# An event loop sets the order of all engines in a two-level matrix product with attention; eight of sixteen steps with seven products in place of seven

## The chip, the cores and the metric

The kernel runs on one core of a Trainium2 chip. The core has a matrix engine (TensorE, PE in the profile, with its weight loads as PEld), a vector engine (VectorE, DVE), a scalar engine (ScalarE, ACT), GpSimd (POOL) and a queue engine (SyncE, SP) that here only issues DMAs. Each engine takes its own instructions in the order of the program, and semaphores make one wait for another. The metric is the time of one execution on the device in microseconds, as a median of several runs.

## The reference

The input is one sequence of 256 tokens with 4096 channels in float32. With the depth of this case only the attention layer runs, and then the final norm:

```python
def attn_branch(xn, w_in, w_out):
    proj = xn @ w_in                       # 256 x 4096 by 4096 x 16384
    q, k, v, g = jnp.split(proj, 4, axis=-1)
    o = stick_breaking_attention(to_heads(q), to_heads(k), to_heads(v))   # 32 heads of 128
    ...
    return (o * jax.nn.silu(g)) @ w_out    # 256 x 4096 by 4096 x 4096

def reference(...):
    h = x
    h = h + attn_branch(rms_norm(h, norm_attn), w_in_attn, w_out_attn)
    return rms_norm(h, final_norm)
```

In the attention every key before a token gets a share of what the keys nearer to the token have left: `sigmoid(z)` times the product of `1 - sigmoid(z)` over the keys between. The reference computes it in log space with a running sum over the keys. Nearly all arithmetic is in the two products with `w_in` and `w_out`, 336 MB of float32 weights that are each used once.

## The kernel before

**Precision.** TensorE works on a float32 format of less precision (F32R in the code). Every operand is therefore split into a high part (a cast on ScalarE, L174) and a low part (the operand less its high part, a subtraction on VectorE, `minus`, L101 and L102), and `mm3` (L402 to L408) makes three matmuls of each product: high by high, high by low, low by high. In this document a *product* is these three matmuls on a block of 128 tokens by 128 channels with 128 channels by 512 columns of weights.

**Units and steps.** A *unit* is a pair of column blocks of 512 each. Units 0 to 15 belong to `w_in`; unit u holds the columns of q and k of two heads in one block and those of the gate and v in the other. Units 16 to 20 belong to `w_out`. A unit runs over the 4096 input channels in 16 *steps* of 256. The weights of a step, four pieces of 128 x 512, lie together in a buffer called `raw` (3 buffers, `RAW_BUFS`), which four DMAs on SP's queue fill (`load`, L147 to L155).

**Seven or eight products.** With two halves of the tokens, two halves of the channels of a step and two column blocks a step is a 2 x 2 by 2 x 2 matrix product of blocks: eight block products, or seven with sums of blocks ahead (Winograd's form of Strassen's scheme). Three kinds of units:

- plain (0, 1 and 16): eight products in every step, four accumulators in PSUM;
- mixed (2 to 15, 17 and 18): seven accumulators that are combined at the unit's end. The steps in `SEVEN` (L41) take seven products, the others eight, which go to four of the seven accumulators (`SEVEN_PARTS` and `EIGHT_PARTS`, L57 to L66);
- single (19 and 20): one column block, four products a step.

Weights come to TensorE in *parts*. A step of eight has two parts of two pieces (1024 columns in the profile's shapes). A step of seven has three such parts and one of one piece (512 columns); ahead of its third part VectorE makes the sums of weights in place, one of 1024 columns at L165 and two of 512 at L168 and L169. `split` (L157 to L177) makes a part's high and low half. There are 5 places for the parts of two (`PAIRS`) and one for those of one piece (`SINGLES`). The token blocks, with their own sums, are built once for `w_in` (`build_xn`, during unit 1) and once for `w_out` (`build_heads`, during unit 16) and stay in SBUF.

**Around the products.** In unit 0 the kernel also reads x for the norm's factor (`x_stats`, L306). Combining the accumulators of a mixed unit takes three copies on ScalarE and seven additions on VectorE (`combine_early` and `combine_late`, L340 to L355); a bank has to be combined before the next unit's first product may write it. While unit u + 1 runs, the two heads of unit u go through their attention: the gate's SiLU (`gate`, L372), transposes (`heads_T`, L390), scores and log-sigmoids (`scores`, L413; four ScalarE operations in a chain at L422 to L425), the running sum as a matmul with a triangle (`weights_of`, L435; two ScalarE operations in a chain at L444 and L445) and the weighted sum of v (`heads_out`, L456). The outputs of the heads go to DRAM (`heads_parts`, L471), as the blocks of unit 16 and after are read from there again. One PSUM bank (`att`) is left for all of this. In units 17 to 20 the finished blocks of the output get the residual and the gain (`evac_out`, L529), and at the end `finish` (L547) scales and stores them.

**What sets the order.** The loop at L671 goes through the parts. Ahead of a part's products it emits the splits of as many later parts as there are places for; behind the last part of a step it runs what a table `todo` holds for this unit and step. The table is written out by hand (L578 to L648): so `heads_T` for head 0 stands at step 2 of the next unit, `scores` at 3, `weights_of` at 5, `heads_out` at 6, `combine_early` at 14 and `combine_late` at 15. The tile framework's scheduler takes the instructions from there and may still move one ahead of another on the same engine.

Of the kernel before, what the change touches and what calls it, by code (L numbers as in the profile page):

```python
# [18 lines left out]
P = 128  # L19
# [21 lines left out]
SEVEN = (2, 4, 6, 8, 10, 12, 13)  # L41
# [3 lines left out]
SINGLES = 1  # L45
# [27 lines left out]

@with_exitstack
def kernel(
# [10 lines left out]
    nc = tc.nc  # L86
# [12 lines left out]
    nc.scalar.preload_act_table_set("natural_log_exp_and_others")  # L99
# [38 lines left out]
    ends, starts = {}, {}  # L138
    for n, p in enumerate(parts):
        for k, (b, *_) in enumerate(p["prods"]):  # L140
            starts.setdefault((p["u"], b), (n, k))
            ends[p["u"], b] = (n, k)


    raw, wh, wl = {}, {}, {}

    def load(q):  # L147
        if q >= len(quads):
            return
        raw[q] = wp.tile([P, 2 * KT, W], F32, tag="raw", name=f"raw{q}", bufs=RAW_BUFS)  # L150
        for k, (w, blocks, s) in enumerate(quads[q]):
            for chunks in ([slice(0, 1), slice(1, 2)] if q == 0 else [slice(0, 2)]):
                to = slice(KT * k + chunks.start, KT * k + chunks.stop)
                for i, c in enumerate(blocks):
                    nc.sync.dma_start(raw[q][:, to, i * CW : (i + 1) * CW], w[c, s][:, chunks, :])  # L155

    def split(n):  # L157
        p = parts[n]
        q = p["quad"]
        if p["i"] == 0 and (n == 0 or parts[n - 1]["quad"] != q):  # L160
            load(q + RAW_BUFS - 1)
        r = raw[q]
        if p["seven"] and p["i"] == 2:

            nc.vector.tensor_tensor(  # L165
                out=r[:, 0:3:2, :], in0=r[:, 0:4:3, :], in1=r[:, 2:3, :].broadcast_to([P, 2, W]), op=ALU.add
            )
            nc.vector.tensor_tensor(out=r[:, 3, :], in0=r[:, 0, :], in1=r[:, 3, :], op=ALU.add)  # L168
            nc.vector.tensor_tensor(out=r[:, 1, :], in0=r[:, 3, :], in1=r[:, 1, :], op=ALU.add)  # L169
        place, size = p["place"], p["size"]  # L170
        tag, bufs = ("w", PAIRS) if size == KT else ("s", SINGLES)
        wh[n] = wp.tile([P, size, W], F32R, tag=tag + "h", name=f"wh{n}", bufs=bufs)
        wl[n] = wp.tile([P, size, W], F32R, tag=tag + "l", name=f"wl{n}", bufs=bufs)
        for c in ([slice(k, k + 1) for k in range(KT)] if n == 0 else [slice(0, size)]):  # L174
            f = r[:, place, :][:, c, :]
            nc.scalar.copy(wh[n][:, c, :], f)  # L176
            minus(wl[n][:, c, :], f, wh[n][:, c, :])  # L177
# [7 lines left out]
    def load_x(i):  # L185
        if i >= NS:
            return
        xs[i] = ap.tile([P, KT, S], F32, tag=("one", "two", "vh", "vl")[i % 4], name=f"xs{i}")
        if i:
            nc.sync.dma_start(xs[i], xT[i])  # L190
            return
        for k in range(KT):
            nc.scalar.dma_start(xs[i][:, k, :], xT[i][:, k, :])
            if k == 0:
                nc.scalar.dma_start(gcol, gain_in)

# [6 lines left out]
    def split_x(i):  # L203

        if i >= NS:
            return
        h, l = new_forms(i, PLAIN_FORMS, "s")
        for c in range(KT):
            g = gcol[:, i * KT + c : i * KT + c + 1]
            hc = h[:, 2 * c : 2 * c + 2, :].rearrange("p a b -> p (a b)")  # L210
            lc = l[:, 2 * c : 2 * c + 2, :].rearrange("p a b -> p (a b)")
            if i == 0:
                nc.vector.tensor_scalar(out=hc, in0=xs[i][:, c, :], scalar1=g, scalar2=None, op0=ALU.mult)  # L213
            else:
                nc.scalar.activation(hc, xs[i][:, c, :], AF.Copy, scale=g)
            nc.vector.scalar_tensor_tensor(  # L216
                out=lc, in0=xs[i][:, c, :], scalar=g, in1=hc.bitcast(F32), op0=ALU.mult, op1=ALU.subtract
            )
        del xs[i]

    def build(i, y, seven, what):

        names = SEVEN_FORMS if i in seven else EIGHT_FORMS
        h, l = new_forms(i, names, what)
        tt = nc.vector.tensor_tensor

        def both(to, f):
            nc.scalar.copy(h[:, to, :], f)
            minus(l[:, to, :], f, h[:, to, :])

        if names is EIGHT_FORMS:
            both(slice(0, 4), y)
            y4 = y.rearrange("p (a b) c -> p a b c", a=KT)
            tt(out=y4[:, :, 0, :], in0=y4[:, :, 0, :], in1=y4[:, :, 1, :], op=ALU.subtract)
            both(slice(4, 6), y4[:, :, 0, :])
            return
        both(slice(0, 1), y[:, 0:1, :])
        both(slice(1, 3), y[:, 2:4, :])
        tt(out=y[:, 3, :], in0=y[:, 1, :], in1=y[:, 3, :], op=ALU.subtract)
        tt(out=y[:, 1, :], in0=y[:, 0, :], in1=y[:, 1, :], op=ALU.subtract)  # L240
        tt(out=y[:, 0, :], in0=y[:, 3, :], in1=y[:, 0, :], op=ALU.subtract)
        tt(out=y[:, 2, :], in0=y[:, 2, :], in1=y[:, 0, :], op=ALU.add)
        both(slice(3, 7), y)
# [3 lines left out]
    def load_xn(i):  # L247
        if i < NS:
            ys[i] = wp.tile([P, 4, P], F32, tag="gh", name=f"xn{i}", bufs=3)
            nc.gpsimd.dma_start(ys[i].rearrange("p a b -> p (a b)"), xT[i].rearrange("p a b -> p (a b)"))  # L250

    def build_xn(i):
        y = ys.pop(i)
        for c in range(KT):
            yc = y[:, 2 * c : 2 * c + 2, :]
            nc.vector.scalar_tensor_tensor(
                out=yc, in0=yc, scalar=gcol[:, i * KT + c : i * KT + c + 1], in1=rs["rows"],
                op0=ALU.mult, op1=ALU.mult,
            )
        build(i, y, SEVEN, "n")  # L260

    load_x(0)
    load(0)
    load_x(1)
    load(1)
    load_x(2)


    idle = ap.tile([P, W], BF16, tag="qkh", name="idle")
# [6 lines left out]
    make_identity(nc, ident)  # L276
# [14 lines left out]
    nc.vector.tensor_copy(neg_tri, tri_f)  # L291
# [14 lines left out]
    def x_stats(i):  # L306
        t, q = divmod(i, NQ)
        w = D // NQ
        xr = wp.tile([P, w], F32, tag="gh", name=f"xr{i}", bufs=3)
        nc.sync.dma_start(xr, x[t * P : (t + 1) * P, q * w : (q + 1) * w])  # L310
        junk = ap.tile([P, w], F32, tag="qkl", name=f"junk{i}")
        nc.scalar.activation(junk, xr, AF.Square, accum_out=ssq_x[:, t, q : q + 1])

    def x_factor():
        tot = cp.tile([P, NT], F32, name="ssq_xt")
        nc.vector.reduce_sum(tot, ssq_x, axis=AX.X)
        nc.vector.tensor_scalar(out=tot, in0=tot, scalar1=1.0 / D, scalar2=EPS, op0=ALU.mult, op1=ALU.add)
        r = cp.tile([P, NT], F32, name="rin_r")
        nc.scalar.activation(r, tot, AF.Ln)
        nc.scalar.activation(r, r, AF.Exp, scale=-0.5)  # L320
        rs["v"] = cp.tile([P, NT], F32, name="rin_v")
        for t in range(NT):
            c = slice(t, t + 1)
            e = newton(r[:, c], tot[:, c], f"rin{t}")
            nc.vector.tensor_tensor(out=rs["v"][:, c], in0=r[:, c], in1=e, op=ALU.mult)
    def x_rows():

        wide = ap.tile([P, NT, P], F32, tag="qkh", name="wide")
        for t in range(NT):
            nc.vector.tensor_scalar(  # L330
                out=wide[:, t, :], in0=ident, scalar1=0.0, scalar2=rs["v"][:, t : t + 1], op0=ALU.mult, op1=ALU.add
            )
        turned = att.tile([P, NT, P], F32, tag="att", name="turned")
        for t in range(NT):
            nc.tensor.transpose(turned[:, t, :], wide[:, t, :], ident)
        rs["rows"] = ap.tile([P, NT, P], F32, tag="al", name="rows", bufs=2)
        nc.scalar.copy(rs["rows"], turned)


    def combine_early(bank, one, two):  # L340

        tt = nc.vector.tensor_tensor
        nc.scalar.copy(two[:, 0, :], bank[1])
        nc.scalar.copy(one[:, 0, :], bank[1])
        tt(out=two[:, 0, :], in0=bank[6], in1=two[:, 0, :], op=ALU.add)
        tt(out=two[:, 1, :], in0=bank[7], in1=two[:, 0, :], op=ALU.add)
        nc.scalar.copy(one[:, 1, :], two[:, 1, :])

    def combine_late(bank, one, two):
        tt = nc.vector.tensor_tensor  # L350
        for t, b in enumerate((2, 4)):
            tt(out=one[:, t, :], in0=bank[b], in1=one[:, t, :], op=ALU.add)  # L352
        for t in (1, 0):
            tt(out=two[:, t, :], in0=bank[5], in1=two[:, t, :], op=ALU.subtract)
        tt(out=two[:, 0, :], in0=bank[3], in1=two[:, 0, :], op=ALU.add)  # L355
# [4 lines left out]
    def new_heads(u):  # L360

        st["qk", u] = ap.tile([P, NT, W], F32, tag="one", name=f"qk_sb{u}")
# [369 lines left out]
```

## Time and profile before

| what | before |
|---|---|
| time, median of 3 runs | 1788.64 us (1787.94 to 1792.77) |
| the profiled execution's own time | 1787.47 us |
| its span, first to last instruction | 1785.8 us |
| mean granted clock of TensorE | 0.996 |
| instructions | 23623 |
| moved by DMA | 388.81 MB |

The span is a little shorter than the time of the same execution, since the time also holds what lies around the first and the last instruction. Times in the rows are microseconds, or ns where a row says "mean ns"; L102 is line 102 of the kernel; `wl<-raw,wh` names what an instruction writes and reads, with buffer numbers left out. `wh` and `wl` are the high and low parts of weights; `sh`, `nh`, `oh`, `ph` and `rh` with their low parts are the token blocks of units 0 and 1, of the mixed units of `w_in`, of unit 16, of the units after it and of the last steps.

### The profile page before, as it was taken

The numbers are of one execution on the slowest core, as the hardware profiler recorded it, in microseconds if no ns is written. First come the engines' busy times: TensorE is split into PE (matmuls) and PEld (weight loads), VectorE is DVE, ScalarE is ACT, GpSimd is POOL, SyncE is SP. The second block draws the span as 40 slices with busy tenths as digits, with TensorE's granted clock in tenths as the row PEclk, the third lists the DMA queues.
The fourth block names the chain that finished last, engine by engine and source line by source line (L and its number), as shares of the span: only waits on it lengthen the run. The fifth ranks groups of instructions, "written<-read, shape, count | busy, mean of one in ns | idle before, by whom it ended". The sixth has DMA issues, their size and how long they took to land.

```text
span 1785.8 us, 23623 instructions
## 1 busy us (share of the span) xinstructions
PE 1765.1 (99%) x8059; PEld 1456.9 (82%) x8059; DVE 1539.7 (86%) x1885; ACT 1122.8 (63%) x1533; POOL 68.5 (4%) x135
## 2 busy tenths in 40 slices
PE   9999999999999999999999999999999999999997
PEld 7887888888888888888888888888888878888886
DVE  6678999989898989899999999989989888999863
ACT  6665666666666666666666666666666666665543
POOL 0001000000000000000000000000002201000000
PEclk9999999999999999999999999999999999999998
DMA  9966666566666666666666666757578978778874
GB/s 314 339 196 217 197 187 212 183 212 186 209 195 200 205 198 205 198 207 196 210 194 212 193 209 189 221 174 229 170 223 266 308 231 248 228 225 264 258 239 157
DMA packets 373993, 388.81 MB, mean 218 GB/s; under 512 B 23856, under 2 KB 351792, under 8 KB 373872
## 3 DMA queue, kind: packets, MB, share of 16 engines
q1 hardware_dynamic: 357296, 352.15, 62.7%
q0 software_dynamic: 14992, 32.78, 5.8%
q10 hardware_dynamic: 1584, 2.38, 0.4%
q8 instruction: 63, 1.03, 0.2%
q14 instruction: 58, 0.48, 0.1%
HBM read 370.43 MB, written 16.78 MB: 217 GB/s over the span
## 4 chain that ended last, share of the span: by engine, by line
PE 81%; issue 7%; DVE 4%; DMA 4%; ACT 3%; SPq 1%; POOL 0%; ACTq 0%; POOLq 0%; DVEq 0%
PE acc L406 26%; PE acc L407 26%; PE acc L408 25%; DVE wl L102 2%; ACT wh L176 2%; DMA xr<-in_x_dram 1%; DMA raw<-in_w_in_dram 1%; SPq L155 1%; PE tr L395 1%; DMA raw<-in_w_out_dram 1%; DMA xn<-in_xT_dram 0%; DVE raw L165 0%; DMA xres<-in_x_dram 0%; PE o L407 0%; PE o L408 0%
## 5 line engine op out<-in xcount | busy, mean ns | idle before, releaser
L102 DVE TENSOR_TENSOR wl<-raw,wh 128x1024 fp32r<-128x1024 f32 (+1 forms) x865 | 973.9, 1150 | 190.1 <-ACT wh L176 182.8
L176 ACT CAST wh<-raw 128x1024 fp32r<-128x1024 f32 (+1 forms) x865 | 833.5, 992 | 440.1 <-DVE raw L165 127.5
L406 PE MATMUL acc<-wh,nh 128*128 128x512 f32 x1694 | 669.0, 395 | 0.9 <-DVE qk_sb L352 0.6
L407 PE MATMUL acc<-wl,nh 128*128 128x512 f32 x1694 | 660.5, 390 | 0.0
L408 PE MATMUL acc<-wh,nl 128*128 128x512 f32 x1694 | 660.3, 390 | 0.0
L408 PEld LDWEIGHTS acc<-wh,nl 128*128 128x128 f32 x1694 | 318.0, 188 | 67.4
L407 PEld LDWEIGHTS acc<-wl,nh 128*128 128x128 f32 x1694 | 318.6, 188 | 63.7 <-DVE wl L102 2.8
L406 PEld LDWEIGHTS acc<-wh,nh 128*128 128x128 f32 x1694 | 318.1, 188 | 63.8 <-ACT wh L176 1.0
L165 DVE TENSOR_TENSOR raw<-raw 128x1024 f32<-128x1024 f32 x112 | 136.4, 1218 | 0.1
L407 PE MATMUL acc<-wl,ph 128*128 128x512 f32 x314 | 122.5, 390 | 0.4 <-DVE wl L102 0.2
L408 PE MATMUL acc<-wh,pl 128*128 128x512 f32 x314 | 122.2, 389 | 0.0
L406 PE MATMUL acc<-wh,ph 128*128 128x512 f32 x314 | 122.2, 389 | 0.0
L406 PE MATMUL acc<-wh,sh 128*128 128x512 f32 x256 | 100.3, 392 | 0.6 <-DVE sh L213 0.6
L408 PE MATMUL acc<-wh,sl 128*128 128x512 f32 x256 | 99.7, 390 | 0.6 <-DVE sl L216 0.6
L407 PE MATMUL acc<-wl,sh 128*128 128x512 f32 x256 | 99.9, 390 | 0.3 <-DVE wl L102 0.3
L168 DVE TENSOR_TENSOR raw<-raw 128x512 f32<-128x512 f32 x112 | 77.2, 689 | 2.7
L169 DVE TENSOR_TENSOR raw<-raw 128x512 f32<-128x512 f32 x112 | 76.9, 687 | 1.8
L407 PEld LDWEIGHTS acc<-wl,ph 128*128 128x128 f32 x314 | 58.9, 188 | 13.7 <-DVE wl L102 1.7
L406 PEld LDWEIGHTS acc<-wh,ph 128*128 128x128 f32 x314 | 58.9, 188 | 12.4
L408 PEld LDWEIGHTS acc<-wh,pl 128*128 128x128 f32 x314 | 58.9, 188 | 12.1
L406 PEld LDWEIGHTS acc<-wh,sh 128*128 128x128 f32 x256 | 48.1, 188 | 11.0 <-issue 1.4
L408 PEld LDWEIGHTS acc<-wh,sl 128*128 128x128 f32 x256 | 48.0, 188 | 11.1 <-DVE sl L216 1.1
(158 smaller groups left out, 1436.0 us busy)
## 6 DMA issues: line engine op xcount, KB each, us to landing
raw<-in_w_in_dram SPq DMA_DIRECT2D x1020, 256.0 KB, 4.5
raw<-in_w_out_dram SPq DMA_DIRECT2D x256, 256.0 KB, 4.4
xr<-in_x_dram SPq DMA_DIRECT2D x16, 256.0 KB, 4.8
xn<-in_xT_dram POOLq DMA_DIRECT2D x16, 256.0 KB, 3.9
spill_f<-gated POOLq DMA_DIRECT2D x16, 256.0 KB, 3.8
spill_h<-oh POOLq DMA_DIRECT2D x16, 256.0 KB, 3.2
spill_l<-ol POOLq DMA_DIRECT2D x16, 256.0 KB, 2.5
oh<-spill_h POOLq DMA_DIRECT2D x16, 256.0 KB, 4.9
```

The costliest lines, as they stand in the source:

```text
L102: nc.vector.tensor_tensor(out=out_, in0=full, in1=part.bitcast(F32), op=ALU.subtract)
L155: nc.sync.dma_start(raw[q][:, to, i * CW : (i + 1) * CW], w[c, s][:, chunks, :])
L165: nc.vector.tensor_tensor(out=r[:, 0:3:2, :], in0=r[:, 0:4:3, :], in1=r[:, 2:3, :].broadcast_to([P, 2, W]), op=ALU.add)
L168: nc.vector.tensor_tensor(out=r[:, 3, :], in0=r[:, 0, :], in1=r[:, 3, :], op=ALU.add)
L169: nc.vector.tensor_tensor(out=r[:, 1, :], in0=r[:, 3, :], in1=r[:, 1, :], op=ALU.add)
L176: nc.scalar.copy(wh[n][:, c, :], f)
L395: nc.tensor.transpose(tr[:, k, t * P : (t + 1) * P], st["qk", u][:, t, c : c + P], ident)
L406: nc.tensor.matmul(out_, ah, bh, start=start, stop=False, **kw)
L407: nc.tensor.matmul(out_, ah, bl, start=False, stop=False, **kw)
L408: nc.tensor.matmul(out_, al, bh, start=False, stop=stop, **kw)
```

## The change

The change replaces the table `todo` and the loop over parts by a plan. Each task (a split of a part, a head's attention, a combine, a load) becomes a Python generator that yields requests: wait until something is told (`until`), take a place in a ring of buffers (`take`), or do a piece of work on an engine (`work`). An event loop runs the generators against a planned clock with a price per instruction. When an engine is free in the plan, it takes of the waiting pieces the one with the earliest due time (`turn`), emits its instructions, and is free again after their price; whoever depends on it goes on after the price and a tail. Products are due at their place in TensorE's order, parts at the place of their first product (the cast 2 us ahead, the sums 3 us), combines at the start of the next unit, and most else 4 us after the latest product. The attention's matmuls go ahead of products once they are ready in the plan. Every instruction is pinned behind the one emitted before on its engine (`keep_in_program_order`), so the framework's scheduler doesn't move it. The sizes change too: `SEVEN` has eight steps, `SINGLES` is 2, the rings of `f` and `al` have one buffer in place of two, the residual `xres` shares the ring `gh` (3 buffers) with other rows, and the norm's factor `rows` takes one of the single places until the token blocks are built.

Each operation stays as it was, with its shape; the calls move into the generators. In the diff, cut to its core, "..." marks what is left out.

```diff
-SEVEN = (2, 4, 6, 8, 10, 12, 13)
+SEVEN = (1,3,5,7,9,11,13,14)
...
-SINGLES = 1
+SINGLES = 2
...
+def vector_ns(n):
+    return 67 + 1.0417 * n
+def scalar_ns(n):
+    return 98 + n / 1.2
+def tensor_ns(n):
+    return 0.4167 * n + 13.4 if n > 128 else 109.0
+class Plan:
+    TAIL = {"tensor": 190, "vector": 114, "scalar": 125, "gpsimd": 50, "sync": 50}
+    LEAD = 195
...
+    def turn(self, engine):
+        if self.free[engine] > self.now or not self.waiting[engine]:
+            return
+        _, _, cost, emit, after, go, hold, moves = heapq.heappop(self.waiting[engine])
+        emit()
+        end = self.now + cost
+        self.free[engine] = end
+        seen = end + self.TAIL[engine]
+        for k, (size, adds) in enumerate(moves):
+            begin = max(self.now + cost * (k + 1) / len(moves) + 1300, self.moved)
+            self.moved = begin + size * (1.78e3 if adds else 0.83e3) / 2**18
+            seen = self.moved + 900
+        if after:
+            self.later(seen, after)
+        self.later(seen if hold else end, go)
+        self.later(end, self.turn, engine)
...
-    nc = tc.nc
+    nc = Plan(tc)
...
+    def soon(c=4.0):
+        return nc.here + 1e3 * c
+    def ten(emit, *n):
+        return nc.work("tensor", sum(tensor_ns(m) for m in n), emit, nc.here - 1e4)
+    def moved(engine, emit, sizes, key, after=None, hold=False, adds=False):
+        issue = {"sync": 55, "gpsimd": 900, "scalar": 90}[engine]
...
+    def sums(q):
+        a, b, c, d = quad_parts[q]
...
+        key = first[c] - 3.0 * 1e3
+        yield nc.until(("lows", a), ("lows", b))
+        yield dve(
+            lambda: tt(
+                out=r[:, 0:3:2, :], in0=r[:, 0:4:3, :], in1=r[:, 2:3, :].broadcast_to([P, 2, W]), op=ALU.add
+            ),
+            2 * W, key,
+        )
+        nc.tell(("sums", c))
+        key = first[d] - 3.0 * 1e3
+        yield dve(lambda: tt(out=r[:, 3, :], in0=r[:, 0, :], in1=r[:, 3, :], op=ALU.add), W, key)
+        yield dve(lambda: tt(out=r[:, 1, :], in0=r[:, 3, :], in1=r[:, 1, :], op=ALU.add), W, key)
+        nc.tell(("sums", d))
+    def piece(n, c, there):
+        p = parts[n]
+        yield nc.until(*there)
+        f = raw[p["quad"]][:, p["place"], :][:, c, :]
+        size = (c.stop - c.start) * W
+        yield act(lambda: nc.scalar.copy(wh[n][:, c, :], f), size, first[n] - 2.0 * 1e3)
+        yield dve(lambda: minus(wl[n][:, c, :], f, wh[n][:, c, :]), size, first[n])
+        for k in range(c.start, c.stop):
+            nc.tell(("low", n, k))
+        low_done(n)
...
+        def soft():
+            nc.scalar.activation(f, z, AF.Abs, scale=scale)
+            nc.scalar.activation(f, f, AF.Exp, scale=-1.0)
+            nc.scalar.activation(f, f, AF.Ln, bias=1.0)
+            nc.scalar.activation(f, f, AF.Copy, scale=1.0 / scale)
+        yield act(soft, (BW,) * 4)
...
+    def products():
+        for g, (n, k) in enumerate(order):
...
+            if starts[u, b] == (n, k):
+                yield nc.take(f"b{b}")
+                ev.setdefault(u, {})[b] = acc.tile([P, W], F32, tag=f"b{b}", name=f"acc{u}_{b}")
+            yield nc.until(("low", n, c), ("form", what, s), lead=nc.LEAD)
+            yield nc.work(
+                "tensor", PRODUCT, lambda: product(n, k), g * PRODUCT, after=lambda n=n, k=k: done(n, k), hold=False
+            )
+            nc.here = g * PRODUCT
```

More of the change, by code (lines that the diff above doesn't have):

```diff
@@ L157, in split @@
-    def split(n):
-        p = parts[n]
[L159 to L177, printed above, removed]
+    n_parts = len(parts)
@@ new lines @@
+    kept = range(n_parts - KEPT, n_parts)
+    order = [(n, k) for n in range(n_parts - KEPT) for k in range(len(parts[n]["prods"]))]
+    for rows in (("A11", "A12"), ("A21", "A22")):
+        order += [(n, k) for n in kept for k, (_, f, _) in enumerate(parts[n]["prods"]) if f in rows]
+    starts, ends, first, left, place_of = {}, {}, {}, {}, {}
+    PRODUCT = 3 * tensor_ns(W)
+    for g, (n, k) in enumerate(order):
+        p = parts[n]
+        b = p["u"], p["prods"][k][0]
+        starts.setdefault(b, (n, k))
+        ends[b] = n, k
+        first.setdefault(n, g * PRODUCT)
+        place_of.setdefault((p["u"], p["s"]), g * PRODUCT)
+        left["step", p["u"], p["s"]] = left.get(("step", p["u"], p["s"]), 0) + 1
+        left["part", n] = left.get(("part", n), 0) + 1
@@ L269, with blocks_all @@
+        yield nc.until(("used", 1, i))
+        yield from build(i, y, SEVEN, "n", key)
+        nc.give("gh")
+    def blocks_all():
+        for i in range(1, NS):
+            if i > 3:
+                yield nc.until(("used", 0, i - 4))
+            nc.start(blocks_of(i))
+    together(blocks_of(0), load(), blocks_all())
+    nc.run(1e3)
     idle = ap.tile([P, W], BF16, tag="qkh", name="idle")
@@ L340, in combine_early @@
[L340 to L355, printed above, removed]
@@ new lines, with heads @@
+    spill = {}
+    def heads(u):
+        together(v_parts(u), gate(u))
+        yield nc.until(("qk", u))
+        for i in range(HG):
+            yield from head(u, i)
+        nc.give("vh", "vl")
+        gated = st["o", u]
+        if u == NS - 1:
+            yield nc.until(("used", NB - 1, u))
+            oh, ol = new_forms(u, PLAIN_FORMS, "o")
+        else:
+            yield nc.take("qkh", "qkl")
+            oh = ap.tile([P, 4, P], F32R, tag="qkh", name=f"oh{u}")
+            ol = ap.tile([P, 4, P], F32R, tag="qkl", name=f"ol{u}")
+        yield act(lambda: nc.scalar.copy(oh, gated), 4 * P)
+        yield dve(lambda: minus(ol, gated, oh), 4 * P)
+        nc.tell(("heads", u))
+        if u == NS - 1:
+            nc.tell(("form", "o", u))
+            return
+        places = ((("gh",), "f", gated), (("qkh",), "h", oh), (("qkl",), "l", ol))
+        for k, (rings, what, t) in enumerate(places):
+            spill[u, what] = dp.tile([P, 4, P], t.dtype, name=f"spill_{what}{u}")
+            yield moved(
+                "gpsimd", lambda: nc.gpsimd.dma_start(spill[u, what], t), [4 * P], soon(),
+                after=lambda rings=rings, k=k: (nc.give(*rings), k == 2 and nc.tell(("spilled", u))),
+            )
@@ L621, in block_out, with count_down, done @@
-    def block_out(c, t):
-        evac_out(c, t, hs[c, t])
-    at(U, 15, plain_h, U, 0)
+    def count_down(*name):
+        left[name] -= 1
+        return not left[name]
+    def done(n, k):
+        p = parts[n]
+        u, s = p["u"], p["s"]
+        if ends[u, p["prods"][k][0]] == (n, k):
+            nc.tell(("full", u, p["prods"][k][0]))
+        if count_down("part", n):
+            nc.give("w" if p["size"] == KT else "s")
+        if count_down("step", u, s):
+            nc.tell(("used", u, s))
@@ new lines, with in_turn @@
+    together(split(KT, "w", PAIRS), split(1, "s", SINGLES), products(), x_stats(), x_factor(), rows_done())
+    def in_turn(works):
+        for w in works:
+            yield from w
+    for i in range(NS):
+        nc.start(rows_of(i))
+    together(*(out_of(u) for u in range(NB)))
+    nc.start(in_turn(heads(u) for u in range(NB)))
+    for s in range(NS - 1):
+        nc.start(load_parts(s, "o", ("used", NB - 1, s)))
+    for s in range(NS):
+        nc.start(build_heads(s))
+    U = OUT0
```

872 lines of the change are left out of this document (579 added, 293 removed).

## Prediction

> **What bounds the kernel now.** I read the page's busy line first, then the span cut into the program's units, then the matmul starts inside one unit, then what TensorE waited for.
>
> ```profile
> span 1785.8 us, 23623 instructions
> ...
> PE 1765.1 (99%) x8059; PEld 1456.9 (82%) x8059; DVE 1539.7 (86%) x1885; ACT 1122.8 (63%) x1533; POOL 68.5 (4%) x135
> ```
>
> TensorE is busy 99% by this line, but its ends are modelled, so the line alone doesn't say that it runs at its own pace. Starts do. They stand in the timeline of TensorE inside a middle unit:
>
> ```profile
> 900.01 0.39 PE L408 MATMUL acc<-wh,nl 128*128 128x512 f32 x1
> 900.24 0.39 PE L406 MATMUL acc<-wh,nh 128*128 128x512 f32 x1
> 900.47 0.39 PE L407 MATMUL acc<-wl,nh 128*128 128x512 f32 x1
> 900.69 0.39 PE L408 MATMUL acc<-wh,nl 128*128 128x512 f32 x1
> ```
>
> A matmul of 512 columns starts every 0.227 us (0.68 us for three), so one product of the program (three matmuls) costs **0.68 us**. (The Trainium skill, "TensorE: Matmul & The Clock Gate", section "Wait — 56ns, not 53.3ns?", has 215.7 ns for a warm matmul of 512; by it a product is 0.65 us. The rows show 0.227 and decide.)
>
> Next the span by units: a row is one unit from its first product to the next unit's first, found by counting products. The columns are length, busy time of PE, PEld, DVE, ACT and POOL, then the granted clock.
>
> ```profile
> core 0: us, PE busy (x) PEld busy (x) DVE busy (x) ACT busy (x) POOL busy (x), PEclk, DMA share, GB/s
> 0.00:5.80 5.80, 3.94 (x9) 1.19 (x9) 1.23 (x3) 1.90 (x2) 1.52 (x10) 1.00 0.61 192
> 5.80:94.90 89.10, 88.14 (x386) 72.11 (x387) 61.14 (x86) 61.82 (x104) 1.76 (x3) 1.00 1.00 327
> 94.90:191.70 96.80, 93.56 (x429) 76.95 (x429) 79.02 (x146) 59.16 (x96) 8.61 (x16) 1.00 0.67 207
> 191.70:280.60 88.90, 88.50 (x408) 72.91 (x407) 81.09 (x96) 60.65 (x83) 1.62 (x3) 1.00 0.64 199
> 808.20:896.20 88.00, 88.00 (x409) 72.94 (x408) 79.46 (x93) 56.98 (x75) 1.61 (x3) 1.00 0.64 200
> 1247.90:1336.60 88.70, 88.09 (x408) 72.76 (x407) 78.64 (x92) 56.99 (x75) 1.61 (x3) 1.00 0.63 198
> 1336.60:1424.90 88.30, 88.28 (x407) 72.96 (x408) 77.93 (x91) 55.45 (x74) 19.12 (x36) 1.00 0.91 284
> 1424.90:1521.40 96.50, 94.65 (x429) 78.00 (x428) 78.68 (x128) 61.44 (x98) 9.14 (x17) 0.98 0.78 246
> 1521.40:1604.60 83.20, 82.90 (x364) 67.97 (x363) 76.92 (x86) 50.15 (x64) 0.00 (x0) 1.00 0.71 222
> 1604.60:1687.30 82.70, 82.61 (x365) 68.07 (x364) 73.68 (x79) 46.10 (x57) 7.40 (x14) 1.00 0.84 262
> 1687.30:1774.50 87.20, 87.17 (x385) 71.85 (x383) 49.88 (x61) 38.04 (x52) 0.00 (x0) 1.00 0.61 194
> 1774.50:1785.80 11.30, 0.00 (x0) 0.00 (x0) 3.79 (x12) 4.18 (x10) 0.00 (x0) 0.59 0.77 285
> ```
>
> The middle row is a mixed unit with attention: 7 steps of seven products and 9 of eight are 121 products, 82.3 us; its 88.0 us leave **5.7 us** for the attention's matmuls. TensorE has no idle time in it at all. So most of the kernel is TensorE at its own pace, and only fewer products can shorten it. The other rows show what else is there to win. A plain unit has 128 products, 87.0 us, and with attention 92.7. Unit 1 takes 96.8, so 4.1 us are lost; unit 16 takes 96.5, so 3.8. Unit 2 loses 0.9, units 14 and 15 lose 0.7 and 0.3, unit 17 (no attention, 82.3 of products) 0.9, unit 18 0.4. Together **11.1 us**. The waits of TensorE in units 1 and 16 and the start of the second wait's end:
>
> ```profile
> PE o L406 <- ACT gated L465: 3.2, 2, 2.4
> PE acc L406 <- DVE gv_sb L355: 1.9, 1, 1.9
> 1430.32 0.50 PE L406 MATMUL acc<-wh,oh 128*128 128x512 f32 x1 [1.85 <-DVE gv_sb L355]
> 1431.60:1435.00 3.40, 3.40 (x10) 2.64 (x9) 2.88 (x4) 3.12 (x6) 0.00 (x0) 0.52 0.72 225
> ```
>
> The first row is a group of attention matmuls that stands in TensorE's queue before its input is there (unit 1); the second a bank that is combined late (unit 16). Behind that wait of 1.85 us the granted clock is 0.52 for 3.4 us, which costs about another 1.7 us. Both are losses of order, not of work.
>
> **The change part by part.** *Eight steps of seven products in place of seven.* There are 16 mixed units, each loses one product: 16 x 0.68 = **-10.9 us** of TensorE. What VectorE pays stands in its timeline:
>
> ```profile
> 899.34 1.22 DVE L102 TENSOR_TENSOR wl<-raw,wh 128x1024 fp32r<-128x1024 f32 x1
> 900.48 0.69 DVE L102 TENSOR_TENSOR vl<-gv_sb,vh 128x512 fp32r<-128x512 f32 x1
> 901.08 1.22 DVE L165 TENSOR_TENSOR raw<-raw 128x1024 f32<-128x1024 f32 x1
> 902.21 0.69 DVE L378 SCALAR_TENSOR_TENSOR gl<-gv_sb,gl 128x512 f32<-128x512 f32 x1
> 903.48 1.23 DVE L102 TENSOR_TENSOR wl<-raw,wh 128x1024 fp32r<-128x1024 f32 x1
> 904.62 0.69 DVE L169 TENSOR_TENSOR raw<-raw 128x512 f32<-128x512 f32 x1
> 905.22 0.69 DVE L380 TENSOR_TENSOR gv_sb<-gv_sb,gl 128x512 f32<-128x512 f32 x1
> DVE wl L102 <- ACT wh L176: 8.0, 8, 1.5
> ```
>
> From start to next start 1024 columns cost 1.14 us and 512 cost 0.60. A step of eight has two low parts of 1024. A step of seven has three, one of 512, the sum at L165 (1.13) and the sums at L168 and L169 (0.60 each): one step more costs VectorE 1.14 + 0.60 + 1.13 + 1.20 = 4.07 us per unit. Its 79.5 us of the middle row become 83.5, and the unit becomes 120 products, 81.6 + 5.7 = **87.3 us**: 96% busy. In unit 17 it is 76.9 + 4.1 = 81.0 of 81.6, 99%, but that row holds work left over from unit 16 that may move ahead. ScalarE gains one cast of 1024 and one of 512; even at VectorE's price for these widths that is 1.7 us on 57.0: covered. So TensorE stays the bound if VectorE's idle time falls to 3.8 us a unit. The last row above (the waits inside 808.2 to 896.2) shows 8.0 us of idle time, all of it VectorE standing at a low part whose cast isn't done.
>
> *The order by an event loop.* It adds no operation to speak of; it decides each engine's next instruction from planned times, earliest due first, and pins it. A low part enters VectorE's queue only when its cast is planned as done, so the 8.0 us should mostly go; attention enters TensorE's queue only when its input is planned as ready, so the 3.2 us of unit 1 should go; combines carry a due time just before the bank is needed, so the 1.9 us and the slow clock behind it should go. I take all **-11.1 us** as going; the other end is 0. The plan's prices fit the rows: 67 + 1.0417 n is 1134 and 600 ns against 1.14 and 0.60, and 0.4167 n + 13.4 is 227 against 0.227.
>
> What the order adds: attention groups now enter TensorE's queue just in time, and whoever is later than planned stops TensorE with every product behind. The surest lateness is in ScalarE's chain of four (its starts, before):
>
> ```profile
> 831.00 0.49 ACT L422 ACTIVATE f<-z 128x384 f32<-128x384 f32 x1
> 831.51 0.53 ACT L423 ACTIVATE f<-f 128x384 f32<-128x384 f32 x1
> 832.07 0.53 ACT L424 ACTIVATE f<-f 128x384 f32<-128x384 f32 x1
> ```
>
> The plan has 98 + 384/1.2 = 418 ns for each of the four; the rows show 0.51 and 0.56, since each reads what the one ahead wrote. So the four are about 0.5 us late, and the pair at L444 and L445 some 0.1: 0.6 us per head, 32 heads, at most 19 us. TensorE takes a new group only between products, 0.68 us apart, so a planned group waits 0.34 us on average anyway, which covers about half. I take **+9 us**, between 0 and 19.
>
> *Two slots for single parts, the residual's rows in another ring, the norm's rows in a single slot.* Memory only, with the same DMAs: I take nothing. A second single slot lets a second low part be made ahead, which can only help; the residual's loads now share three slots with the gains, and if they came late the combine of units 17 and 18 would wait, which has a whole unit of time. The queue of loads:
>
> ```profile
> 1515.86 2.50 SPq L155 DMA_DIRECT2D raw<-in_w_out_dram  x4
> raw<-in_w_in_dram SPq DMA_DIRECT2D x1020, 256.0 KB, 4.5
> ```
>
> Four issues take 2.50 us and the last lands 4.5 us after it starts, some 6.4 us from the first; the plan's terms (0.22 + 1.3 + 4 x 0.83 + 0.9) give 5.7. So a cast may be due 0.7 us before its weights are there, and behind it on ScalarE's queue stand attention operations. Cover: three buffers for weights, so a load is issued about two steps (10.9 us) before its use. I take nothing; were the cover gone, 0.7 us for each load that is waited for, which is inside the 19 us up to some 27 loads.
>
> *Sum.* The profiled execution took 1787.5 us (span 1785.8 and 1.7 around it): 1787.5 - 10.9 - 11.1 + 9 = 1774.5. The median of the runs is 1.2 higher, so I predict **1776 us**. Start (5.8), unit 0, the two single units (87.2) and the tail (11.3) stay.
>
> **The rivals.**
>
> *VectorE becomes the bound (slower).* Place: the low parts at L102 in the 14 mixed units with attention. It has 87.3 - 83.5 = 3.8 us to spare where it now idles 8.0. Above 4.5 us of waits a unit is longer than today's 88.0. If all 8.0 stay, a unit is 91.5, +3.5 x 14 = 49 us: 1838; if 6 us stay, 89.5, +21: 1810. For it: all engines take their instructions in order, and 99% in unit 17. Against it: the wait is one of order (a cast that stands behind L165 or L169), which is what the plan looks at, and the lead of five pair parts is about two steps.
>
> *Just-in-time groups stop TensorE (no change or slower).* Five groups a head are 160. 22 us of gain are spent at 0.14 us a group: 1788, no change; at 0.3 us, half of the worst lateness at each, 48 us are lost: 1815. For it: before, these groups had slack of whole steps. Against it: a stop of TensorE lets the others catch up, so lateness isn't paid at each group. A page's rule bears on it: the Trainium skill, "TensorE: Matmul & The Clock Gate", section "What's actually happening", has the clock halved after an idle window of some 3.4 us, by which short stops cost only themselves. The trace disagrees: 1.85 us of waiting was enough once (0.52 granted), while the longest wait of unit 1, 2.4 us, left that unit at 1.00. By the rule this rival's prices stand; by the row each stop of about 2 us may cost 1.7 more.
>
> *Only the products go (faster, less).* The new order's waits equal the old ones': 1788.6 - 10.9 = 1778. *The change doesn't do what it says:* the product is saved but its matmuls are replaced by idle time before the two extra parts; then units stay at 88.0 and 1788 remains.
>
> **How the numbers follow.** The forecast and the case of only the products lie between 1766 (no new wait: 1788.6 - 22) and 1783: 0.60. No change (a measurement can't tell 0.3%, 5.4 us, from none; 1783 to 1794): 0.13, half from groups, half from a product replaced by idle time. Slower: VectorE 0.13, groups 0.14, together 0.27. To leave out no more than 2 in 10 the range runs from 1765 to 1812, over the middle price of both slower rivals.
>
> **What would show it.** Right: mixed units of 87.3 to 87.8 us, unit 1 and unit 16 near 92.7, VectorE 95% busy in a unit with its waits for the cast under 3 us, no clock below 1.00 inside. Waits of TensorE for ScalarE or VectorE in attention groups, 0.1 to 0.4 us each and 9 us in all, would show the added term. Wrong: mixed units over 88 us; TensorE waiting for low parts (VectorE the bound); waits of many groups summing to more than 20 us; loads landing after the cast is due.

## The result and the profile after

The changed kernel takes 1801.43 us (median of 7 runs, 1795.85 to 1805.19), the kernel before 1789.24 beside it: ratio 1.0065, 95% interval 1.0048 to 1.0082. It is **slower by 0.65%** where 1776 us was forecast. The profiled execution has a span of 1803.4 us. Its page, and its units (same columns as before; each row runs from a unit's first product to the next one's):

```profile
PE 1768.4 (98%) x8011; PEld 1450.0 (80%) x8011; DVE 1611.2 (89%) x1974; ACT 1145.4 (64%) x1568; POOL 67.0 (4%) x132
```
```profile
5.90:98.00 92.10, 91.27 (x390) 74.80 (x391) 59.01 (x84) 62.23 (x106) 1.76 (x3) 1.00 0.97 317
98.00:190.90 92.90, 92.90 (x430) 76.95 (x430) 83.18 (x150) 61.57 (x99) 8.63 (x16) 1.00 0.74 227
546.60:635.40 88.80, 88.11 (x407) 72.34 (x406) 84.86 (x100) 58.97 (x78) 1.61 (x3) 1.00 0.65 204
1345.70:1434.30 88.60, 87.99 (x405) 72.20 (x404) 83.15 (x97) 56.70 (x76) 19.11 (x36) 1.00 0.90 273
1434.30:1533.90 99.60, 95.94 (x425) 78.78 (x424) 76.12 (x127) 61.58 (x98) 6.46 (x12) 0.97 0.71 223
1533.90:1616.80 82.90, 82.23 (x361) 67.43 (x360) 78.54 (x90) 49.77 (x62) 0.00 (x0) 1.00 0.69 210
1616.80:1704.80 88.00, 84.33 (x361) 66.87 (x360) 80.79 (x87) 48.12 (x59) 8.49 (x16) 1.00 0.80 251
```

The 48 matmuls are gone (8011 for 8059), and unit 1 takes 92.9 us, near the 92.7 that were hoped for. But a mixed unit takes 88.8 us where 87.3 were due, unit 0 loses 3.0 us more than before, unit 16 takes 99.6 and unit 18 88.0. From the first mixed unit to unit 16 (190.9 to 1434.3) the fourteen mixed units take 1243.4 us, before 1233.2: +10.2 us, where fourteen products fewer (-9.5) and the end of their old losses (-1.9) were due. What stopped TensorE:

```profile
PE tr L106 <- DVE qk_sb L106: 11.0, 12, 1.5
PE acc L106 <- DVE wl L106: 4.0, 5, 1.0
PE z L106 <- ACT fh L106: 1.7, 1, 1.7
```

(All operations go through one helper now, so all have line 106; read them by tiles.) The longest sum is new: the attention's first transposes, put into TensorE's queue just in time, stand there until the late combine of q and k is done. That names the victim. The cause stands two engines further back. The waits of ScalarE's cast for weights, and one such stop followed back through the timelines of SP, ScalarE, VectorE and TensorE:

```profile
ACT wh L106 <- DMA raw<-in_w_in_dram: 121.0, 80, 3.7
ACT wh L106 <- DMA raw<-in_w_out_dram: 33.0, 21, 3.5
```
```profile
519.58 5.38 SPq L106 DMA_DIRECT2D raw<-in_w_in_dram  x8
525.89 2.53 ACT L106 CAST wh<-raw 128x512 fp32r<-128x512 f32 x3 [3.69 <-DMA raw<-in_w_in_dram]
...
544.35 0.62 ACT L106 CAST wh<-raw 128x512 fp32r<-128x512 f32 x1 [2.17 <-DMA raw<-in_w_in_dram]
544.87 0.61 ACT L106 COPY qk_sb<-gv_sb 128x512 f32<-128x512 f32 x1
545.52 0.69 DVE L106 TENSOR_TENSOR qk_sb<-acc,qk_sb 128x512 f32<-128x512 f32 x1 [0.82 <-ACT qk_sb L106]
546.26 0.55 PE L106 MATMUL tr<-ident,qk_sb 128*128 128x128 f32 x3 [1.29 <-DVE qk_sb L106]
```

The first two rows show the lead. The first holds the loads of two steps, four issues each. The cast at 525.89 stood 3.69 us for the fourth load of the first of them, which landed at 525.79, about 6 us after the step's first issue at 519.58. It uses the load on landing. The last four are one stop. ScalarE stands 2.17 us at another cast until its load has landed; the copy of q and k is queued behind that cast and starts at 544.87, though VectorE's last addition into `gv_sb` ahead of it, the tile that it reads, had ended by 543.57; VectorE's last addition of the combine waits 0.82 us for the copy; the transposes wait 1.29 us for the addition, with every product behind them in TensorE's queue. The row of TensorE names VectorE, that of VectorE ScalarE, and only ScalarE's names the load. Waits of the cast for loads alone prove nothing, though: they sum to 154 us here, but to 84 us in the kernel before, where middle units lose nothing.

### The profile page after: what moved, and what is told of

Its sections match the earlier page's. It is cut to its first block, busy times and chain, and to the rows that moved or that the text cites. A ratio compares the mean times of both kernels' runs of the same rounds, so it can differ in the third digit from the quotient of the medians.

```text
span 1803.4 us, 23678 instructions
## 1 busy us (share of the span) xinstructions
PE 1768.4 (98%) x8011; PEld 1450.0 (80%) x8011; DVE 1611.2 (89%) x1974; ACT 1145.4 (64%) x1568; POOL 67.0 (4%) x132
## 4 chain that ended last, share of the span: by engine, by line
PE 63%; DVE 13%; DMA 10%; ACT 6%; issue 4%; SPq 3%; ACTq 0%; DVEq 0%
PE acc L106 59%; DMA raw<-in_w_in_dram 6%; DVE wl L106 6%; ACT wh L106 5%; DVE raw L106 4%; SPq L106 3%; DMA raw<-in_w_out_dram 3%; PE z L106 2%; PE o L106 1%; DVE gv_sb L106 1%; PE tr L106 1%; ACT f L106 0%; ACT qk_sb L106 0%; ACT h L106 0%; ACTq L106 0%
## 5 line engine op out<-in xcount | busy, mean ns | idle before, releaser
L106 ACT CAST wh<-raw 128x1024 fp32r<-128x1024 f32 (+1 forms) x898 | 857.5, 986 | 478.5 <-DVE raw L106 221.4
L106 DVE TENSOR_TENSOR wl<-raw,wh 128x1024 fp32r<-128x1024 f32 (+1 forms) x898 | 1003.1, 1142 | 138.5 <-ACT wh L106 124.0
L106 DVE TENSOR_TENSOR raw<-raw 128x512 f32<-128x512 f32 (+1 forms) x384 | 332.6, 866 | 6.8
L106 PE MATMUL acc<-wh,pl 128*128 128x512 f32 x304 | 118.4, 389 | 0.0
L106 PEld LDWEIGHTS acc<-wl,sh 128*128 128x128 f32 x256 | 48.9, 191 | 9.9
L106 ACT CAST qkh<-tr 128x512 fp32r<-128x512 f32 x32 | 18.8, 588 | 56.6 <-PE tr L106 56.5
```

What stands on the lines that cost most here:

```text
L106: return self.tc.keep_in_program_order(getattr(self.engine, name)(*args, **kw))
```

## The experiments

Theories: **(1)** the eighth step is too much for VectorE, in any order; **(2)** the order is at fault: attention enters TensorE's queue too early, since chained ScalarE operations are priced too low; **(3)** loads land later than the plan believes (with its terms the last of four loads lands some 5.7 us after the first issue; in the trace of after the median of this is 6.8 us in mixed units, worked out from issues and landings, and in the kernel before 6.7: the loads became no slower, the plan expected them too early), and each lateness runs from ScalarE over VectorE to TensorE.

**order_seven.** `SEVEN = (2, 4, 6, 8, 10, 12, 13)` in the changed kernel.

> The event loop's order with the old seven steps of seven products (the steps of before). Products cost 10.9 us more than in the changed kernel. If the eighth step is what overloads VectorE and the loads (first theory), the stops of TensorE fall from some 40 us to under 15 and the time is 1778 to 1790, below before (1789). If the order itself is at fault (second theory: groups of attention matmuls due too early by the plan's prices, whatever the steps), the stops stay and the time is about 1801 + 10.9 = 1812.

Measured 1792.12 us, ratio to before 1.0013 (1.0000 to 1.0025): between the two answers, near no change. TensorE's own waits fall from some 22 us to some 11, as the first answer had it, but the time doesn't fall below before. Middle units lose nothing; units 1 and 16 win 3.8 and 4.3 us on before, and units 0, 15 and 18, all with a high DMA share (0.97, 0.89 and 0.80), lose 2.9, 2.7 and 4.5. A middle unit, then units 15 and 18:

```profile
545.70:633.60 87.90, 87.90 (x409) 72.94 (x408) 80.57 (x93) 57.63 (x75) 1.61 (x3) 1.00 0.64 201
1338.00:1429.00 91.00, 88.78 (x408) 72.81 (x407) 80.16 (x92) 57.03 (x75) 19.12 (x36) 1.00 0.89 271
1604.30:1691.50 87.20, 83.73 (x365) 67.84 (x364) 75.66 (x81) 47.49 (x58) 7.43 (x14) 1.00 0.80 246
```

**old_eight.** `SEVEN = (1, 3, 5, 7, 9, 11, 13, 14)` in the kernel before.

> The old hand-written order with the new eight steps of seven products, one place for single parts as before. First theory (the eighth step doesn't fit in what VectorE and the loads have left, in any order): the 10.9 us of products come back as stops, mixed units of 88 us or more, 1789 to 1805. Second theory (only the new order is at fault): units of 87.3 us and 1776 to 1780.

Measured 1868.83, ratio 1.0444 (1.0426 to 1.0463). The loss is far more than either answer had. The longest wait of TensorE is for the early combine (L352), which stands at step 14, now a step of seven:

```profile
PE acc L406 <- DVE qk_sb L352: 36.3, 13, 4.6
```

The hand-written order with one place for single parts can't carry these eight steps. Whether the order or the place is missing isn't shown by this run, as the changed kernel brings both.

**loads.** Two prices of the plan, nothing else:

```diff
-        issue = {"sync": 55, "gpsimd": 900, "scalar": 90}[engine]
+        issue = {"sync": 640, "gpsimd": 900, "scalar": 90}[engine]
-            seen = self.moved + 900
+            seen = self.moved + (1600 if engine == "sync" else 900)
```

> The changed kernel with the plan's price of a load on SP's queue set to what the trace shows (0.64 us to issue each, landing 0.7 us later), nothing else. If late loads are what pushes VectorE and ScalarE behind the plan (third theory), the plan makes room for them, the waits of the cast for a load stop pushing TensorE, and the time falls by 12 to 25 us, to 1776 to 1790. If the stops come from ScalarE's chains or from VectorE's load alone it stays within 5 us of 1801.

Measured 1777.06, ratio 0.9933 (0.9920 to 0.9947): **24 us faster than the changed kernel**, and faster than before. The cast's waits for loads fall from 154 us to 26:

```profile
ACT wh L106 <- DMA raw<-in_w_in_dram: 17.2, 24, 2.0
ACT wh L106 <- DMA raw<-in_w_out_dram: 8.8, 13, 2.2
540.40:628.60 88.20, 88.20 (x410) 72.80 (x409) 83.63 (x98) 58.57 (x78) 1.61 (x3) 1.00 0.63 198
628.60:715.90 87.30, 87.21 (x401) 71.94 (x400) 84.05 (x98) 57.99 (x77) 1.61 (x3) 1.00 0.66 204
```

Every second mixed unit of `w_in` now has the forecast 87.3, the others some 88.2. VectorE has the same work in them as in the changed kernel. The new prices also move other instructions, so this run alone can't tell early loads from a better order.

**chain.** The two chains of ScalarE priced 0.42 and 0.14 us longer (`(BW,) * 4 + (48,) * 3` and `(BW, BW, 48)`).

> The changed kernel with the plan's price of the chained ScalarE operations (four and two per head) raised by 0.14 us for each that reads what the one ahead wrote, nothing else. If those chains are the cause (the added term of the prediction, 0.6 us a head), the groups of the running sum and of the output come later in TensorE's queue and the time falls by 8 to 15 us, to 1786 to 1793. If late loads or VectorE's load are the cause: 1797 to 1803.

Measured 1793.17, ratio 1.0028 (1.0017 to 1.0039): 8 us by the medians, 6.6 by the two ratios to before: at or just under the lower end of what theory (2) expected. So the chains have a part, in an order that is late anyway.

**half_issue.** Neither order nor price is touched. The weights are laid out so that the two column pieces of a block lie side by side, and one DMA of 512 KB takes the place of two of 256 KB:

```diff
-                    todo.append([
-                        (raw[q][:, to, i * CW : (i + 1) * CW], w[c, s][:, chunks, :]) for i, c in enumerate(blocks)
-                    ])
+                    c = blocks[0] // 2 if w is w_out else blocks[0] if blocks[0] < NB else blocks[0] - 2 * NB
+                    todo.append([(raw[q][:, to, :], w[c, s][:, chunks, :])])
```

> The changed kernel with its order and prices as they are, but the weights laid out so that one DMA of 512 KB brings what two of 256 KB brought: two issues a step in place of four, so the last load should land about 1.2 us earlier than its 6.8 us after the first issue. Third theory (loads later than the plan expects push ScalarE and VectorE behind it): the hardware now comes near the plan's 5.7 us and the time falls by 15 to 27 us, to 1774 to 1786, without a new price. If the repriced run was faster for another reason (a luckier order): within 5 us of 1801.

Measured **1766.10 us, ratio 0.9870 (0.9857 to 0.9884)**: 35 us faster than the changed kernel, more than the 15 to 27 expected, and the fastest of all runs. The two traces have the same instructions in the same order on TensorE, VectorE, ScalarE and GpSimd, so a luckier order is ruled out. The loads now land a median of 5.0 us after the first issue, inside the plan's 5.7:

```profile
raw<-in_w_in_dram SPq DMA_DIRECT2D x510, 512.0 KB, 4.2
```
```profile
538.40:625.70 87.30, 87.30 (x406) 72.48 (x405) 84.14 (x99) 59.05 (x78) 1.61 (x3) 1.00 0.55 202
1411.90:1504.10 92.20, 92.20 (x426) 76.58 (x425) 77.16 (x132) 62.22 (x99) 6.46 (x12) 1.00 0.66 239
1504.10:1585.70 81.60, 81.60 (x362) 67.57 (x361) 79.08 (x88) 50.29 (x63) 0.00 (x0) 1.00 0.61 222
1585.70:1667.30 81.60, 81.60 (x362) 67.57 (x361) 79.31 (x87) 49.06 (x59) 8.49 (x16) 1.00 0.78 264
```

Units of 87.3, 92.2 and 81.6 us, with TensorE busy throughout: from unit 1 on every unit is at TensorE's own pace or within 0.2 us of it (unit 0 still takes 90.2). VectorE is 96% busy in a mixed unit and stops nobody, which ends theory (1); the chains are still priced too low and attention groups stop TensorE no more, which leaves theory (2) no part of its own where loads land in time.

**old_half.** The control: the kernel before with the same layout of weights.

> The kernel before, order and steps as they were, with one DMA of 512 KB in place of two of 256 KB. Third theory: before, TensorE never waited for weights in a middle unit, so earlier loads can only take a few of the 11 us lost in other units: 1780 to 1789. If the larger DMA is faster for every order (less issuing, better transfers), the 35 us that it gave the changed kernel show here in good part: under 1775.

Measured 1790.45, ratio 1.0009 (1.0001 to 1.0018), just above the first answer. It is a net: unit 16 takes 3.2 us less than before and units 2, 14, 15 and 17 together 2.3 less, but unit 0 takes 2.1 more and unit 1 6.5 more, with a wait of 5.0 us in its attention. Units 1 and 16:

```profile
98.00:201.30 103.30, 95.55 (x430) 78.56 (x429) 79.37 (x146) 59.81 (x97) 8.60 (x16) 0.97 0.55 195
1432.70:1526.00 93.30, 93.26 (x430) 76.78 (x429) 76.83 (x126) 60.06 (x96) 9.16 (x17) 1.00 0.71 246
```

The middle units stay at 87.9 us. Larger DMAs alone don't bring the 35 us; these belong to the order that needs its loads early.

**loads_seven.** The prices of *loads* with the old seven steps.

> The event loop with the load's price corrected and the old seven steps. If the eighth step is worth its 10.9 us once the order is right, this is 1783 to 1788 (the repriced kernel with eight steps has 1777). If the eighth step gives its products back as stops on weights, this is level with it or faster: 1772 to 1778.

Measured 1782.86, ratio 0.9966 (0.9953 to 0.9978). With loads rightly priced the eighth step is worth 5.8 us of its 10.9 (1777.06 against 1782.86), at these places of the steps.

**loads_h8.** Both prices, steps of seven at 2, 4, 6, 8, 9, 11, 13, 14.

> The event loop with both prices corrected (loads and ScalarE's chains) and eight steps of seven at other places: 2, 4, 6, 8, 9, 11, 13, 14. In the repriced kernel every second mixed unit still loses 0.8 us and unit 18 1.7 us. If these are steps of seven standing too near for the three buffers of weights, the other places free them: 1768 to 1774. If the eighth step can't be had for less: 1776 to 1782.

Measured 1772.01, ratio 0.9900 (0.9885 to 0.9916): 5 us less than *loads*. Two things differ from *loads*, the places of the steps and the price of the chains; which of them gave the 5 us isn't shown.

**old_eight_13.** The old order with steps 1, 3, 5, 7, 9, 11, 12, 13. It has three steps of seven in a row, which I overlooked.

> The old hand-written order with eight steps of seven, but the last of them at step 13, as before, so that the early combine at step 14 finds its banks full. If the place of the last step of seven cost the 79 us (the early combine and what stands behind it on VectorE's queue wait for step 14's last products), the time is 1778 to 1795. If the eighth step's VectorE work doesn't fit in the old order wherever it stands: 1820 to 1870.

Measured 1859.87, ratio 1.0389 (1.0375 to 1.0404). TensorE's waits for the early combine fall from 36.3 us to 6.4, and waits for weights stand in their place (L176 is the line of the cast):

```profile
PE acc L406 <- ACT wh L176: 27.6, 33, 1.1
PE acc L407 <- DVE wl L102: 11.2, 17, 1.5
```

**old_eight_half.** The same with one DMA in place of two.

> The old order with eight steps of seven (the last at step 13) and one DMA of 512 KB in place of two. If late loads are what the old order, too, loses with eight steps: 1776 to 1790. If it is the order written by hand (parts and combines standing in line on ScalarE and VectorE at the end of a unit): little changes against 1860, 1840 to 1862.

Measured 1847.62, ratio 1.0330 (1.0316 to 1.0344): 12 us of the 70. Late loads aren't the main loss of the old order with one place for single parts.

**half_single.** *half_issue* with `SINGLES = 1`, the norm's rows in a slot of their own.

> The changed kernel with one DMA in place of two (1766) and only one place for single parts, the norm's rows in a slot of their own. If the second place carries the eighth step (a low part of 512 columns made ahead while TensorE still uses the last), stops on weights come back in the steps of seven: 1775 to 1800. If it does little: 1766 to 1769.

Measured 1841.22, ratio 1.0294 (1.0280 to 1.0308): 75 us, a miss by far; I took the second place for a small help. The stops stand at the pair of neighbouring steps of seven, 13 and 14, and the clock drops behind them (the unit's row has 0.98):

```profile
819.88 0.50 PE L106 MATMUL acc<-wl,nh 128*128 128x512 f32 x1 [0.50 <-DVE wl L106]
821.89 0.51 PE L106 MATMUL acc<-wh,nh 128*128 128x512 f32 x1 [0.59 <-ACT wh L106]
823.88 0.70 PE L106 MATMUL acc<-wl,nh 128*128 128x512 f32 x1 [1.49 <-DVE wl L106]
740.10:832.70 92.60, 90.02 (x406) 73.34 (x405) 83.97 (x99) 58.01 (x77) 1.61 (x3) 0.98 0.54 190
```

By the kernel's code the reason is this: with one place the single part of step 14 can't be made before the third product of step 13 is done, and the sums that overwrite `raw` wait for it. So cast, low part, sum, cast and low part stand in one chain within seven products, 4.8 us. It also puts *old_eight* in another light: with one place the event loop loses nearly as much as the old order (1841 against the 1848 of *old_eight_half*, both with large DMAs, though with other steps of seven).

**old_eight_two** and **old_eight_two_half.** The old order with the change's eight steps, two single places and the residual in the ring `gh`; the second with one DMA in place of two.

> The old order written by hand, the changed kernel's eight steps of seven and its two places for single parts (the residual's rows share the ring of three, as in the change). If the place is what the eighth step needs and the hand-written order is good enough: 1776 to 1792, level with or below before. If the old order can't carry eight steps (parts, combines and attention standing in line on VectorE and ScalarE): 1815 to 1865.

> The same with one DMA of 512 KB in place of two of 256 KB. If place and early loads are all that the eighth step needs: 1766 to 1780, near the event loop's 1766. If the order is needed as well: 1800 to 1855.

Measured 1876.17, ratio 1.0475 (1.0452 to 1.0499), and 1802.72, ratio 1.0072 (1.0057 to 1.0088). The second place alone only moves the wait. ScalarE now stands 177 us for loads, and TensorE stands 49.7 us for `gated`, an attention operation on ScalarE's queue. With large DMAs both fall together. Rows of the first, then of the second kernel:

```profile
PE o L406 <- ACT gated L465: 49.7, 30, 4.0
ACT wh L176 <- DMA raw<-in_w_in_dram: 176.9, 121, 5.3
```
```profile
PE o L406 <- ACT gated L465: 9.4, 7, 3.1
ACT wh L176 <- DMA raw<-in_w_in_dram: 48.5, 52, 3.6
```

Place and early loads together take 66 us off the old order's 1869; the event loop's order, with the few smaller rings that came with it, is worth the remaining 37 us to 1766. So 1766 needs all three: the second place, the order, and loads that land when the order expects them. The last can be had in part without larger DMAs, by right prices: *loads* and *loads_h8* reach 1777 and 1772.

## Why the prediction was wrong

The step that failed is the one on the queue of loads: "Cover: three buffers for weights, so a load is issued about two steps (10.9 us) before its use. I take nothing". It had the plan's 5.7 us beside the rows' 6.4 and named the cast that would be due too early, and then covered it with a lead that isn't there. In the fourteen mixed units of `w_in` the first cast of a step starts a median 8.1 us after the step's first issue (before: 9.8) and only 0.7 us after the last of its four loads has landed (before: 3.2; matched from the order of casts and loads in the traces). A buffer comes free when the last low part of its step is made, and only then is the next load issued. In the passage from 519.58 us above, all that was loaded had been cast by 522.2 us, so the next load was due on landing. That term was worth 35 us (*half_issue*), where I took 0 and allowed up to 27 late loads inside the 19 us; the cast waited for a load 101 times. The miss of 25 us is about these 35 less the 9 that I had added for just-in-time groups.

The direction was wrong too: faster was forecast, slower came. That 1801 lies inside the range given, up to 1812, is luck: the upper end came from the prices of the two slower rivals, and neither is what happened. Two of the signs that were named for a wrong forecast came as named, mixed units over 88 us and loads landing after the cast is due.

Point by point:
- *Products, -10.9*: right. In *half_issue* mixed units are at 87.3 us, and units 17 and 18 at 81.6.
- *VectorE 96% busy and no bound*: right in size and verdict; 84.1 us of 87.3 in *half_issue* against the 83.5 worked out. The rival that made it the bound had the wrong engine.
- *Losses of order, -11.1*: right as possible (they are gone in *half_issue*), wrong as taken: only unit 1's 4 us went in the changed kernel, unit 16 and unit 18 got worse.
- *Just-in-time groups, +9*: that attention groups stop TensorE was right, the place and cause were mostly wrong. The running sum behind ScalarE's chain stood 2.6 us in all, the transposes 11.0. Underpriced chains were worth 7 to 8 us on top of late loads; in *half_issue* they are priced as low, and no attention group stops TensorE.
- *The last of four loads lands 6.4 us after the first issue*: about right; the trace of before has a median of 6.7.
- *Two slots for single parts, nothing*: wrong too, though it didn't show: one place costs 75 us with eight steps. It went unseen because the change brings the place.
- The rival of groups that stop TensorE named "no change or slower" at 0.14 to 0.3 us a group; the time came out between the two, but by late loads: right prices for them give 24 us back, earlier issues 35.

Open: why the longer price of the chains alone gave 7 to 8 us (it may only have left room for late loads), what unit 0 loses (90 us or more with the event loop, 89.1 before, where 87.0 is TensorE's pace), and why the changed kernel's runs spread over 9.3 us where those of *half_issue* spread over 1.8.

## What to carry to other kernels

An order that is computed to the last tenth of a microsecond is as good as its worst price: check every price of a plan against the trace, DMA issue and landing first, since in-order engines hand each lateness on. A ring of buffers is a lead only if its places are full of finished loads; look at what the engine does when a load lands (a wait that ends with the landing means no lead). When a stop names an engine, follow that engine's own waits back before blaming it.

## What the runs showed of the hardware

Behind stops of TensorE the clock drops, and not by the length of one stop alone. In the changed kernel two stops of 1.67 and 0.89 us at the attention of unit 16 were followed by more than 5 us at about half:

```profile
1449.80 0.44 PE L106 MATMUL z<-fh,neg_tri 128*128 128x384 f32 x1 [1.67 <-ACT fh L106]
1451.13 0.69 PE L106 MATMUL z<-fl,neg_tri 128*128 128x384 f32 x1 [0.89 <-DVE fl L106]
1451.30:1457.70 6.40, 6.40 (x18) 5.17 (x19) 4.64 (x12) 3.32 (x8) 0.54 (x1) 0.52 0.76 253
```

Whether such a drop comes differs between stops of the same length. In *half_single* each of the fourteen mixed units of `w_in` has one stop of 1.49 or 1.50 us. Behind nine of them matmuls ran 0.43 us apart for some 2 to 3 us, behind five they didn't. Units with the drop take 92.4 to 92.7 us, those without it 90.9 or 91.0, so the drop cost about as much again as the stop. Such a unit stands under *half_single*; one without the drop:

```profile
556.40:647.40 91.00, 88.44 (x405) 72.22 (x404) 83.89 (x98) 58.01 (x77) 1.61 (x3) 1.00 0.54 192
```

At the start of the changed kernel matmuls run 0.43 us apart until 13.6 us (2.4 us of unit 0's loss from 8.5 on) while the granted clock is given as 1.00; the starts show what the clock's column doesn't:

```profile
9.36 0.63 PE L106 MATMUL acc<-wh,sl 128*128 128x512 f32 x1
9.79 0.63 PE L106 MATMUL acc<-wh,sh 128*128 128x512 f32 x1
9.00:13.00 4.00, 4.00 (x11) 3.13 (x10) 2.73 (x5) 1.52 (x3) 0.00 (x0) 1.00 0.99 282
```

No stop near 2 us stands ahead of this slow start, and *half_issue* has one as well, until 10.7 us; in the kernel before most matmuls run 0.23 us apart from the first product on. What makes the difference isn't shown.
